# Query and key of differential heads: in the core, or by way of DRAM

## The chip, the cores and the metric

The kernel runs on one core of one Trainium2 chip. The time is device microseconds of one execution; runs are compared by their median. The engines named here are TensorE (PE), VectorE (DVE), ScalarE (ACT), GpSimd (POOL) and SyncE (SP), which issues all DMAs of this kernel.

## What is computed

Two layers over 1040 tokens (16 meta tokens and 1024 inputs), model width 1024. In each layer a normalised input is projected into two groups of heads: four differential pairs (two maps of width 64 each, with partial rotary embedding) and eight forgetting heads (no rotary):

```python
def partial_rope(t, cos, sin):          # ROT_DIM = 16 of HEAD_DIM = 64
    half = ROT_DIM // 2
    t1, t2, tp = t[..., :half], t[..., half:ROT_DIM], t[..., ROT_DIM:]
    ...
    return jnp.concatenate([t1 * cos - t2 * sin, t2 * cos + t1 * sin, tp], axis=-1)
...
dq = partial_rope(dq.reshape(b, lp, DIFF_HEADS, 2, HEAD_DIM), cos, sin)
dk = partial_rope(dk.reshape(b, lp, DIFF_HEADS, 2, HEAD_DIM), cos, sin)
...
p = jax.nn.softmax(s, axis=-1)
a = p[:, :, 0] - lam * p[:, :, 1]       # the two maps of a pair
```

So of the 128 rows of q or k of a pair only 2 x 16 are rotated; the other 96 pass as they are. Each pair's output is normalised, gated by a SiLU path, and all heads go through one output projection that is added to the residual.

## The kernel before

**Tiling.** Tokens lie along the free axis in three chunks of 336, 384 and 320 (`CS`, `CE`), and in nine blocks for attention. All float32 products are made of float32r parts: an operand is split into a high part (a rounded copy, on ACT) and a low part (the rest, on DVE), and a projection tile (`mtile`) is 24 matmuls: eight k tiles times high x high, low x high, high x low. A score sums two products: k's tile holds the highs of one map in its 64 rows and the lows in the other 64, `qq` holds q's highs twice (the second copy by POOL, L477), `ql` the lows.

**Units.** A layer's side work is cut into units: `k_unit`, `q_unit` and `gate` (one pair, three chunks, one `mtile` each), `v_unit` (two pairs, nine blocks of 24 matmuls). `attention` goes pair by pair (0 to 3 differential, 4 to 7 forgetting), chunk by chunk: scores, softmax, transposes, products with v. PE's order is set by a planner: `ORDER` lists the units, `fills` runs them as filling between the steps of `attention`, and due times tell it how long after its last matmul a tile may be used (`LROT`, 8.0 us for rotated ones, `LFOX` for the others, in `when`). The other engines' and SP's order is set by the framework's scheduler, engine by engine, from the same program; each engine, and SP, takes its list in order.

**Rotation** (`rotate`, L407 to 422), once per unit and chunk on 128 rows: a DMA of a full table of cosines and sines (L413), a copy out of PSUM on ACT (L416), a shuffle that swaps the halves of the rotated rows (DVE, L418), the product with the sines (POOL, L419), the product with the cosines and the add (DVE, L420, L421); rows that aren't rotated meet a one and a zero. Then `split` by halves of 64 rows (L426, L428).

**Buffers.** `WB` 8 converted weight tiles, `XB` 4 staging tiles for loaded weights (`load_w`, L244: 128 KB each, high on ACT or POOL, low on POOL or DVE), `QB` 8 q tiles, `GB` 4 kept gates, `TCB` 3 work tiles. The output projection (`out_main`) loads its weights again for each chunk: 8 x 3 x 4 loads a layer. PSUM has two banks for projections (`pj`), three for scores (`sc`).

## Time and profile before

| | us |
|---|---|
| median of 3 runs (lowest, highest) | 1605.58 (1605.05, 1609.21) |
| the profiled execution's own time | 1607.66 |
| its span, first to last instruction | 1605.6 |
| PE busy in the span | 1487.7 |
| DVE busy | 1043.0 |

The mean granted clock of PE is 0.973 of full speed. Durations below come from the one profiled execution. A span leaves out 2.1 us of the execution's own time. Busy time of PE is modelled from pipelined matmuls, so what counts is where it sits idle and what ended that. The differential pairs of layer 0 lie at 86 to 350 us, those of layer 1 at 850 to 1140; forgetting heads, output projection and the next layer's first units follow each.

### The profile page before, as it was taken

Reading aid. Unit: us, or ns where it says so; the run is one execution under the profiler, and the core shown is the slowest. Engines: PE = TensorE matmul, PEld = TensorE weight load, DVE = VectorE, ACT = ScalarE, POOL = GpSimd, SP = SyncE. Lnnn points to the kernel's source line nnn. Section 1 sums busy time; section 2 is a strip of 40 time slices with the busy share of each in tenths; the row PEclk is TensorE's granted clock in tenths of the full one; section 3 lists DMA queues with packets and bytes.
Section 4 is the critical chain, followed back from the end, with each engine's and each line's share of the span. In section 5 each row is a group of like instructions: output and inputs, shape, how many; then the busy total and the mean of one; then the engine's idle time right before and its main releaser. Section 6 shows DMA issues by size and latency. Waiting matters only on the chain. (4 is left out here: it accounts for less than half of the span.)

```text
span 1605.6 us, 30162 instructions
## 1 busy us (share of the span) xinstructions
PE 1487.7 (93%) x9932; PEld 1420.1 (88%) x9932; DVE 1043.0 (65%) x3024; ACT 828.6 (52%) x2067; POOL 689.6 (43%) x1125
## 2 busy tenths in 40 slices
PE   5988999999999999988998999899999999888997
PEld 4888989999999999887988899799999999886897
DVE  6488747866755575757655976586756555547564
ACT  6455545545654565543334654465556556446443
POOL 3353233404442445456846341442253344344674
PEclk9999999999999999998999999999999999999999
DMA  9252212223321324555434231332242222335454
GB/s 242 64 113 73 71 51 75 72 36 86 69 66 42 79 67 126 170 151 159 147 70 106 69 87 33 88 81 50 43 93 59 52 69 61 87 96 159 138 158 139
DMA packets 181725, 148.28 MB, mean 92 GB/s; under 512 B 19624, under 2 KB 177120, under 8 KB 181568
## 3 DMA queue, kind: packets, MB, share of 16 engines
q1 hardware_dynamic: 181568, 146.34, 34.6%
q8 instruction: 79, 1.29, 0.3%
q14 instruction: 78, 0.64, 0.1%
...
## 5 line engine op out<-in xcount | busy, mean ns | idle before, releaser
L179 PE MATMUL pj<-acth,whi 128*128 128x320 f32 (+2 forms) x1536 | 517.0, 337 | 22.9 <-ACT tc L416 7.6
L179 PE MATMUL pj<-acth,wlo 128*128 128x320 f32 (+2 forms) x1536 | 498.1, 324 | 2.7 <-POOL wlo L263 2.7
L179 PE MATMUL pj<-actl,whi 128*128 128x320 f32 (+2 forms) x1536 | 497.8, 324 | 0.0
L263 POOL TENSOR_TENSOR wlo<-wst,whi 128x256 fp32r<-128x256 f32 (+1 forms) x320 | 249.3, 788 | 244.0 <-ACT whi L259 216.3
L179 PEld LDWEIGHTS pj<-acth,whi 128*128 128x128 f32 x1536 | 295.9, 193 | 28.0 <-ACT tc L416 8.2
L179 PEld LDWEIGHTS pj<-acth,wlo 128*128 128x128 f32 x1536 | 295.2, 192 | 3.8 <-POOL wlo L263 3.2
L179 PEld LDWEIGHTS pj<-actl,whi 128*128 128x128 f32 x1536 | 293.9, 191 | 0.0
L660 ACT ACTIVATE e<-e,mn 80x80 f32<-80x80 f32 (+8 forms) x288 | 225.2, 782 | 124.2 <-DVE mn L652 121.6
L744 DVE TENSOR_TENSOR atl<-tp,ath 128x320 fp32r<-128x320 f32 (+8 forms) x432 | 191.5, 450 | 97.7 <-ACT ath L743 92.9
L743 ACT ACTIVATE ath<-tp 128x320 fp32r<-128x320 f32 (+8 forms) x432 | 167.6, 403 | 138.2 <-PE tp L183 131.1
L179 PE MATMUL sc<-kt,qq 128*128 128x296 f32 (+9 forms) x480 | 178.8, 375 | 25.2 <-DVE mn L652 17.3
L259 ACT ACTIVATE whi<-wst 128x256 fp32r<-128x256 f32 (+1 forms) x304 | 124.1, 415 | 150.4 <-DMA wst<-in_w_out_dram 50.7
L693 POOL TENSOR_SCALAR e<-e,rl 80x80 f32<-80x80 f32 (+2 forms) x144 | 110.8, 770 | 165.6 <-DVE rl L692 160.2
L183 PE MATMUL tp<-ident,e 128*128 128x128 f32 (+2 forms) x1080 | 180.7, 275 | 0.9 <-POOL e L693 0.8
L179 PE MATMUL po<-ath,v 128*128 128x256 f32 (+5 forms) x576 | 167.1, 331 | 13.2 <-ACT ath L743 9.9
L179 PE MATMUL pj<-whi,acth 128*128 128x256 f32 (+3 forms) x576 | 166.4, 289 | 6.7 <-DVE v L428 5.8
L179 PE MATMUL pj<-wlo,acth 128*128 128x256 f32 (+3 forms) x576 | 164.2, 285 | 2.1 <-POOL wlo L263 1.4
L179 PE MATMUL pj<-whi,actl 128*128 128x256 f32 (+3 forms) x576 | 163.8, 284 | 0.6 <-POOL actl L404 0.6
L179 PE MATMUL sc<-kt,ql 128*128 128x296 f32 (+9 forms) x480 | 159.7, 335 | 0.0
L179 PE MATMUL po<-atl,v 128*128 128x256 f32 (+5 forms) x432 | 136.8, 317 | 12.8 <-DVE atl L744 11.7
L183 PEld LDWEIGHTS tp<-ident,e 128*128 128x128 f32 (+2 forms) x1080 | 137.1, 140 | 7.0 <-POOL e L693 2.3
L179 PEld LDWEIGHTS sc<-kt,qq 128*128 128x128 f32 (+1 forms) x480 | 91.5, 191 | 37.7 <-DVE mn L652 23.8
...
## 6 DMA issues: line engine op xcount, KB each, us to landing
wst<-in_w_in_dram SPq DMA_DIRECT2D x256, 128.0 KB
wst<-in_w_out_dram SPq DMA_DIRECT2D x192, 128.0 KB
...
```

The lines of the kernel that those rows point to most:

```text
L179: nc.tensor.matmul(o, a, b, start=start, stop=stop)
L183: nc.tensor.transpose(o, a, idn)
L259: nc.scalar.activation(hi, sg_, AF.Copy)
L263: eng.tensor_tensor(lo, sg_, hi.bitcast(F32), ALU.subtract)
L660: nc.scalar.activation(e[rows, :ext], e[rows, :ext], AF.Exp, scale=-1.0, bias=mn[rows, len(pcs) - 1:len(pcs)], accum_out=l[rows, :])
L693: nc.gpsimd.tensor_scalar(e[rows, :ext], e[rows, :ext], r[rows, 0:1], 1.0, ALU.mult, ALU.mult)
L743: nc.scalar.activation(ah[:kz, n0:w], tp[:kz, n0:w], AF.Copy)
L744: nc.vector.tensor_tensor(al[:kz, n0:w], tp[:kz, n0:w], ah[:kz, n0:w].bitcast(F32), ALU.subtract)
```

## The change

For pairs 0 to 3 `k_unit` and `q_unit` hand over to a new `diff_unit`. Per chunk it copies the tile out of PSUM, stores its 2 x 16 raw rotated rows to DRAM (`rscr`), splits all 128 rows at once into highs and lows (`ks`), and stores the 2 x 48 rows that aren't rotated to DRAM (`qkscr`). When q and k of a pair both have a chunk, `rotate` loads their 64 raw rows into one tile, rotates and splits these alone, and stores them to `qkscr` in eight DMAs. `diff_loads` then loads k (four DMAs; chunk by chunk for pair 0, whole for the others), `qq` (two) and `ql` (two) from there. The table for 64 rows is laid out in DRAM once (`rtab`, eight copies). The planner has new due times (`LROT` 9.0, `LBACK` 2.5 after it), another `ORDER`, and `log_forget` is placed by `LLF`. q of the differential heads no longer skips 16 columns in layer 1. Buffers: `XB` 3, `QB` 6 (in pairs), `GB` 2, `TCB` 4, `KB` 2 new.

```diff
-WB, XB, QB, EB, AB, GB, OB, TCB = 8, 4, 8, 6, 2, 4, 3, 3
+WB, XB, QB, EB, AB, GB, OB, TCB, KB = 8, 3, 6, 6, 2, 2, 3, 4, 2
...
-ORDER = ("k0 q0 k1 q1 | g0 k2 v1 q2 | g1 k3 q3 | g2 v2 k4 q4 | g3 k5 q5 | g4 v3 h k6 q6 | k7 q7 g5 | "
+ORDER = ("k0 q0 k1 q1 | k2 q2 v1 | g0 k3 q3 | k4 v2 q4 | g1 g2 k5 q5 | g3 v3 h k6 q6 | g4 k7 q7 g5 | "
          "g6 g7")
...
-LS, LSC, LT, L1S, LROT, LFOX = ((1.9, 0.0033), (3.4, 0.0042)), 0.7, 2.4, 4.87, 8.0, 5.61
+LS, LSC, LT, L1S, LFOX = ((1.9, 0.0033), (3.4, 0.0042)), 0.7, 2.4, 4.87, 5.61
+LTO, LROT, LBACK = 4.0, 9.0, 2.5
+LLF = 8.0
...
-SHUF = list(range(8, 16)) + list(range(8)) + list(range(16, 32))
+SHUF = list(range(8, 16)) + list(range(8)) + list(range(24, 32)) + list(range(16, 24))
...
+        for r in range(0, P, 16):
+            dma(out=rtab[r:r + 16], in_=rope[0:16])
...
-    def rotate(pt, c, scale, o=0):
-        a, b = CS[c] + o, CE[c]
-        w = b - a
-        rt = sb.tile([P, T], F32, name="cb", tag="cb", bufs=2)[:, 0:2 * w]
+    def rotate(l, g, c):
+        a, b = CS[c], CE[c]
+        w, n = b - a, 32 * len(ROPED[g])
+        rt = sb.tile([P, T], F32, name="cb", tag="cb", bufs=2)[:n, 0:2 * w]
         rt = rt.rearrange("p (x w) -> p x w", x=2)
-        dma(out=rt, in_=rope[:, :, a:b])
-        t = st("tc", CW)
-        v = t[:, o:o + w]
-        nc.scalar.activation(v, pt[:, o:o + w], AF.Copy, scale=scale)
-        t2 = st("tc", CW)
-        nc.vector.stream_shuffle(t2[:, :w], v, SHUF)
-        nc.gpsimd.tensor_tensor(t2[:, :w], t2[:, :w], rt[:, 1, :], ALU.mult)
+        dma(out=rt, in_=rtab[:n, :, a:b])
+        v, t2 = st("tc", CW)[:n, :w], st("tc", CW)[:n, :w]
+        dma(out=v, in_=rscr[l, g][:, a:b])
+        nc.vector.stream_shuffle(t2, v, SHUF)
+        nc.gpsimd.tensor_tensor(t2, t2, rt[:, 1, :], ALU.mult)
         nc.vector.tensor_tensor(v, v, rt[:, 0, :], ALU.mult)
-        nc.vector.tensor_tensor(v, v, t2[:, :w], ALU.add)
-        return t
+        nc.vector.tensor_tensor(v, v, t2, ALU.add)
+        split(t2.bitcast(F32R), v.bitcast(F32R), v)
+        for r in range(0, n, 16):
+            i, m = divmod(r // 16, 2)
+            for x, t in enumerate((t2, v)):
+                dma(out=qkscr[l, g][i, 64 * m:64 * m + 16, x, a:b], in_=t[r:r + 16, :])
+    def diff_unit(l, u, acts, box):
+        scale, c0 = (-SCALE, DQ) if u[0] == "q" else (1.0, DK)
+        c0 += int(u[1]) * P
+        g, i = WHERE[u]
+        ws = load_w_all(w_in[l], [(c0, c0 + P)])
+        for c in range(3):
+            a, b = CS[c], CE[c]
+            w = b - a
+            mb = []
+            yield from mtile(ws, acts, c, mb)
+            pt = mb[0][:, :w]
+            v = st("tc", CW)
+            nc.scalar.activation(v[:, :w], pt, AF.Copy, scale=scale)
+            for m in range(2):
+                dma(out=rscr[l, g][32 * i + 16 * m:32 * i + 16 * m + 16, a:b],
+                    in_=v[64 * m:64 * m + 16, :w])
+            parts = sb.tile([P, 2, CW], F32R, name="ks", tag="ks", bufs=KB)[:, :, :w]
+            split(parts[:, 0, :], parts[:, 1, :], pt, scale)
+            for m in range(2):
+                r = slice(64 * m + 16, 64 * m + 64)
+                dma(out=qkscr[l, g][i, r, :, a:b], in_=parts[r].bitcast(F32))
+            box["to", u, c] = pe.t + LTO
+            if all(("to", x, c) in box for x in ROPED[g]):
+                rotate(l, g, c)
+                box["at", g, c] = pe.t + LROT
+            diff_loads(l, box)
+            yield
+    def diff_loads(l, box):
+        while box["lk"] < 12:
+            p, c = divmod(box["lk"], 3)
+            g, i = WHERE[f"k{p}"]
+            if ("at", g, c if p == 0 else 2) not in box or box.get("sp", 0) < p - 1:
+                break
+            if c == 0:
+                box["kt"] = [big("kt", 4, F32R) for _ in range(2)]
+            cols = slice(CS[c], CE[c]) if p == 0 else slice(0, T)
+            if p == 0 or c == 0:
+                for s in range(2):
+                    for x in range(2):
+                        dma(out=box["kt"][s][halves(s)[x], cols].bitcast(F32),
+                            in_=qkscr[l, g][i, halves(s)[0], x, cols])
+                box["lt"] = max(pe.t, box["at", g, c if p == 0 else 2]) + LBACK
+            box["k", p, c] = box["kt"]
+            when["k", p, c] = box["lt"]
+            box["lk"] += 1
+        while box["lq"] < 12:
+            p, c = divmod(box["lq"], 3)
+            g, i = WHERE[f"q{p}"]
+            if ("at", g, c) not in box or p and (p - 1, c) not in box["sc_ok"]:
+                break
+            a, b = CS[c], CE[c]
+            qq = sb.tile([P, 2, CW], F32R, name="qq", tag="qq", bufs=QB // 2)
+            ql = qls[c]
+            for r in halves(0):
+                dma(out=qq[r, :, 0:b - a].bitcast(F32),
+                    in_=qkscr[l, g][i, :, 0, a:b].rearrange("(m d) w -> d m w", d=HD))
+            for s in range(2):
+                r = halves(s)[0]
+                dma(out=ql[s][r, :].bitcast(F32), in_=qkscr[l, g][i, r, 1, a:b])
+            box["q", p, c] = ([qq[:, s, :] for s in range(2)], ql)
+            when["q", p, c] = max(pe.t, box["at", g, c]) + LBACK
+            box["lq"] += 1
...
-            src = rotate(mb[0], c, 1.0) if diff else mb[0]
             for s in range(2):
                 r, ro = halves(s)
-                split(kt[s][r, a:b], kt[s][ro, a:b], src[r, :w])
+                split(kt[s][r, a:b], kt[s][ro, a:b], mb[0][r, :b - a])
...
-            while box["kept"] >= GB:
+            while box["kept"] >= (GB - 1 if p == 7 and c else GB):
```

**SP at pair 0.** SP's list before, from the last table of k0 on: `cb` is the table, `wst` a staging tile of weights.

```order
L413 DMA cb_940<-in_rope_dram 128x2x320
L413 DMA cb_1002<-in_rope_dram 128x2x336
L252 DMA wst_1411<-in_w_in_dram 128x2x128
L252 DMA wst_1417<-in_w_in_dram 128x2x128
L252 DMA wst_1423<-in_w_in_dram 128x2x128
L252 DMA wst_1429<-in_w_in_dram 128x2x128
L413 DMA cb_1044<-in_rope_dram 128x2x384
L413 DMA cb_1086<-in_rope_dram 128x2x320
L413 DMA cb_1211<-in_rope_dram 128x2x336
```

SP's list now, from the raw rows of q0's chunk 0 on (`r00` and `s00` are layer 0, pair 0; `tc` rotated rows, `ks` the others):

```order
L461 DMA r00_111<-tc_1005 16x336 x2
L467 DMA s00_103<-ks_1009 96x1x336 x2
L434 DMA tc_1016<-r00_111 64x336
L461 DMA r00_111<-tc_1069 16x384 x2
L432 DMA cb_1140<-rtab_119 64x2x320
L467 DMA s00_103<-ks_1073 96x1x384
L444 DMA s00_103<-tc_1017 16x336 x2
L444 DMA s00_103<-tc_1016 16x336 x2
L444 DMA s00_103<-tc_1017 16x336
L444 DMA s00_103<-tc_1016 16x336
L444 DMA s00_103<-tc_1017 16x336
L444 DMA s00_103<-tc_1016 16x336
```

Before, SP only brought tables and weights; now its list holds stores, a load that waits for them, and stores that wait for the rotation, and behind these stand `kt` (four), `qq` (two) and `ql` (two).

**SP at pair 3.** SP's list before, at the last tables of q3 and the first weights of v2 (`ta` and `oscr` belong to attention's outputs and gates):

```order
L252 DMA wst_3856<-in_w_in_dram 128x2x128
L786 DMA oscr_100<-ta_3269 128x336
L252 DMA wst_3862<-in_w_in_dram 128x2x128
L620 DMA oscr_100<-ta_3184 128x320
L413 DMA cb_3560<-in_rope_dram 128x2x320
L413 DMA cb_3668<-in_rope_dram 128x2x336
L252 DMA wst_4081<-in_w_in_dram 128x256
L252 DMA wst_4081<-in_w_in_dram 128x8
```

SP's list now, from the loads of chunk 1 to the last transfer ahead of chunk 2's rotated rows:

```order
L507 DMA ql10_87<-s03_106 64x384
L503 DMA qq_3767<-s03_106 64x2x384 x2
L507 DMA ql11_88<-s03_106 64x384
L461 DMA r03_114<-tc_3820 16x320 x2
L467 DMA s03_106<-ks_3824 96x1x320 x2
L434 DMA tc_3831<-r03_114 64x320
L268 DMA wst_4046<-in_w_in_dram 128x2x128
L268 DMA wst_4341<-in_w_in_dram 128x256
L268 DMA wst_4341<-in_w_in_dram 128x8
L268 DMA wst_4348<-in_w_in_dram 128x256
L268 DMA wst_4348<-in_w_in_dram 128x8
L710 DMA oscr_100<-ta_3883 128x336
```

The raw rows of chunk 2 stand behind chunk 1's loads, and weights and a gate's store between them and their own rotated rows; k of pair 3 (`kt`) comes behind all of it.

**DVE at pair 3.** DVE's list before, around q3's rotations of chunks 0 and 1 (`e`, `mn` are scores, `atl` lows of transposes):

```order
L418 STREAM_SHUFFLE tc_3672<-tc_3670 128x336
L712 SCALAR_TENSOR_TENSOR e_3581<-e_3626,rl_3638,e_3581 128x976
L420 TENSOR_TENSOR tc_3670<-tc_3670,cb_3668 128x336
L421 TENSOR_TENSOR tc_3670<-tc_3670,tc_3672 128x336
L803 COPY ms_809<-sc_3727 128x1
L418 STREAM_SHUFFLE tc_3714<-tc_3712 128x384
L803 COPY ms_809<-sc_3727 128x1 x2
L428 TENSOR_TENSOR ql00_85<-tc_3670,qq_3677 64x336
L420 TENSOR_TENSOR tc_3712<-tc_3712,cb_3710 128x384
L428 TENSOR_TENSOR ql01_86<-tc_3670,qq_3678 64x336
L744 TENSOR_TENSOR atl_3739<-tp_3734,ath_3738 80x320
L744 TENSOR_TENSOR atl_3747<-tp_3742,ath_3746 128x320
```

DVE's list now, around the rotations of chunks 1 and 2 (L705 empties the tiles of gate g1):

```order
L437 TENSOR_TENSOR tc_3750<-tc_3750,cb_3748 64x384
L438 TENSOR_TENSOR tc_3750<-tc_3750,tc_3751 64x384
L516 TENSOR_TENSOR tc_3750<-tc_3750,tc_3751 64x384
L518 SCALAR_TENSOR_TENSOR ks_3824<-pj_3795,ks_3824 128x320
L435 STREAM_SHUFFLE tc_3832<-tc_3831 64x320
L705 SCALAR_TENSOR_TENSOR tc_3910<-tc_3910,pj_3885 128x336
L437 TENSOR_TENSOR tc_3831<-tc_3831,cb_3829 64x320
L705 SCALAR_TENSOR_TENSOR tc_3942<-tc_3942,pj_3917 128x384
L438 TENSOR_TENSOR tc_3831<-tc_3831,tc_3832 64x320
L516 TENSOR_TENSOR tc_3831<-tc_3831,tc_3832 64x320
L705 SCALAR_TENSOR_TENSOR tc_3974<-tc_3974,pj_3949 128x320
L742 ISA e_3979,mn_3980<-sc_3981,dm0_69 80x80
```

The rotations have moved from among scores and transposes to the gate's three tiles, whose evictions now stand behind the shuffle of rows that come by DMA. On PE the three tiles of g1 (72 matmuls) are what stands between q3's last tile and the first score of pair 3; before, it was q3's own chunk 1 and half of chunk 2.

## Rows read from the trace of the kernel before

**Rows 1.** The page's part 1: busy us, share of span, instructions by engine.
```profile
PE 1487.7 (93%) x9932; PEld 1420.1 (88%) x9932; DVE 1043.0 (65%) x3024; ACT 828.6 (52%) x2067; POOL 689.6 (43%) x1125
```

**Rows 2.** Busy time by stretch: length; five engines; then clock, DMA share, GB/s.
```profile
86.00:350.00 264.00, 244.79 (x1645) 235.71 (x1644) 197.43 (x583) 139.12 (x354) 90.51 (x131) 0.98 0.29 70
...
850.00:1140.00 290.00, 268.91 (x1822) 260.42 (x1821) 209.52 (x629) 150.54 (x383) 102.57 (x161) 0.98 0.28 69
```

**Rows 3.** Waits of PE over the run: us in total, times, longest.
```profile
PE sc L179 <- DVE mn L652: 17.3, 15, 3.8
...
PE pj L179 <- ACT tc L416: 7.6, 2, 5.5
```

**Rows 4.** Groups by line: operands, count | busy us, mean ns | idle before.
```profile
L419 POOL TENSOR_TENSOR tc<-tc,cb 128x320 f32<-128x320 f32 (+2 forms) x48 | 57.8, 1204 | 66.0 <-issue 41.2 <-DVE tc L418 20.8 <-POOL qq L477 1.8
...
L420 DVE TENSOR_TENSOR tc<-tc,cb 128x320 f32<-128x320 f32 (+2 forms) x48 | 34.4, 717 | 2.7 <-DMA cb<-in_rope_dram 1.9
...
L421 DVE TENSOR_TENSOR tc<-tc 128x320 f32<-128x320 f32 (+2 forms) x48 | 29.7, 619 | 16.9 <-POOL tc L419 16.1
...
L428 DVE TENSOR_TENSOR kt<-tc,kt 64x336 fp32r<-64x336 f32 (+2 forms) x48 | 26.5, 552 | 5.2 <-ACT kt L426 3.9
L418 DVE STREAM_SHUFFLE tc<-tc 128x320 f32<-128x320 f32 (+2 forms) x48 | 26.2, 547 | 0.6
...
L426 ACT ACTIVATE kt<-tc 64x336 fp32r<-64x336 f32 (+2 forms) x48 | 23.5, 490 | 25.6 <-DVE tc L421 24.9
...
L416 ACT ACTIVATE tc<-pj 128x320 f32<-128x320 f32 (+2 forms) x48 | 21.8, 455 | 20.2 <-PE pj L179 19.4 <-DVE kt L428 0.3
```

**Rows 5.** Instructions in order of time, 82 to 92 us: start, length, engine, line.
```profile
83.72 0.45 ACT L416 ACTIVATE tc<-pj 128x336 f32<-128x336 f32 x1 [0.28 <-DVE kt L428]
...
86.11 0.54 DVE L418 STREAM_SHUFFLE tc<-tc 128x336 f32<-128x336 f32 x1
...
86.78 1.16 POOL L419 TENSOR_TENSOR tc<-tc,cb 128x336 f32<-128x336 f32 x1 [1.33 <-DVE tc L418]
...
87.19 1.12 DVE L420 TENSOR_TENSOR tc<-tc,cb 128x336 f32<-128x336 f32 x1
...
89.92 1.19 DVE L428 TENSOR_TENSOR ql<-tc,qq 64x336 fp32r<-64x336 f32 x2 [0.55 <-ACT qq L426]
```

**Rows 6.** SyncE's issues in order of time, 384 to 389 us.
```profile
386.14 0.34 SPq L577 DMA_DIRECT2D cscr<-cb  x1
387.95 0.83 SPq L819 DMA_DIRECT2D cb<-cscr  x2
```

**Rows 7.** SyncE's issues in order of time, 540 to 552 us.
```profile
545.69 3.56 SPq L895 DMA_DIRECT2D nscr<-msr  x12
```

**Rows 8.** The chain of waits that ended last: start, length, what.
```profile
1467.39 2.34 DMA oscr<-ta
...
1523.84 3.37 DMA tc<-nscr
...
1549.34 2.23 DMA wst<-in_w_out_dram
...
1583.28 10.55 PE pj L179 x72
```

**Rows 9.** PE's instructions in order of time, 737 to 744 us.
```profile
740.21 0.69 PE L179 MATMUL pj<-acth,whi 128*128 128x384 f32 x1 [1.90 <-DVE hc L930]
...
742.94 0.52 PE L179 MATMUL pj<-actl,whi 128*128 128x384 f32 x1
743.26 0.52 PE L179 MATMUL pj<-acth,whi 128*128 128x384 f32 x1
```

**Rows 10.** Groups by line, 700 to 760 us: the weights' conversions.
```profile
L263 POOL TENSOR_TENSOR wlo<-wst,whi 128x256 fp32r<-128x256 f32 x22 | 17.2, 785 | 10.6 <-ACT whi L259 9.5 <-DMA wst<-in_w_out_dram 0.9
...
L261 POOL TENSOR_SCALAR whi<-wst 128x256 fp32r<-128x256 f32 x20 | 9.6, 485 | 8.7 <-DMA wst<-in_w_out_dram 6.5 <-DVE tc L914 0.6 <-ACT tc L938 0.5
L259 ACT ACTIVATE whi<-wst 128x256 fp32r<-128x256 f32 x21 | 8.7, 416 | 19.8 <-DMA wst<-in_w_out_dram 9.1 <-PE pj L179 7.2 <-POOL whi L261 2.7
```

More of the change, by code (lines that the diff above doesn't have):

```diff
@@ L157, in trunk_kernel @@
     cscr = dr.tile([depth, 8, T], F32, name="cscr")
+    qkscr = {(l, g): dr.tile([len(us), P, 2, T], F32, name=f"s{l}{g}")
+             for l in range(depth) for g, us in enumerate(ROPED)}
+    rscr = {(l, g): dr.tile([32 * len(us), T], F32, name=f"r{l}{g}")
+            for l in range(depth) for g, us in enumerate(ROPED)}
+    rtab = dr.tile([P, 2, T], F32, name="rtab")
     class Clock:
@@ L378, in first_turn @@
                 tr(pt[:, o:o + n], xts[b][:n, k * P:(k + 1) * P], ident[:n, :n])
-            h = hc_view(hc, c, k) if hc else st("qq", CW, F32, QB)[:, 0:w]
+            if not hc and k % 2 == 0:
+                two = sb.tile([P, 2, CW], F32, name="qq" if k < QB else "ks",
+                              tag="qq" if k < QB else "ks", bufs=QB // 2 if k < QB else KB)
+            h = hc_view(hc, c, k) if hc else two[:, k % 2, 0:w]
             nc.scalar.activation(h, pt[:, :w], AF.Copy)
@@ L435, in k_unit @@
     def k_unit(l, p, acts, box):
-        diff = p < 4
-        k0 = (DK if diff else FK) + (p % 4) * P
+        if p < 4:
+            yield from diff_unit(l, f"k{p}", acts, box)
+            return
+        k0 = FK + (p % 4) * P
         while box.get("sp", 0) < p - 1:
@@ L444, in k_unit @@
             a, b = CS[c], CE[c]
-            w = b - a
             mb = []
             yield from mtile(ws, acts, c, mb)
-            src = rotate(mb[0], c, 1.0) if diff else mb[0]
             for s in range(2):
                 r, ro = halves(s)
-                split(kt[s][r, a:b], kt[s][ro, a:b], src[r, :w])
+                split(kt[s][r, a:b], kt[s][ro, a:b], mb[0][r, :b - a])
             box["k", p, c] = kt
-            when["k", p, c] = pe.t + (LROT if diff else LFOX)
+            when["k", p, c] = pe.t + LFOX
             yield
     def q_unit(l, p, acts, box):
-        diff = p < 4
-        q0 = (DQ if diff else FQ) + (p % 4) * P
+        if p < 4:
+            yield from diff_unit(l, f"q{p}", acts, box)
+            return
+        q0 = FQ + (p % 4) * P
         ws = load_w_all(w_in[l], [(q0, q0 + P)])
@@ L463, in q_unit @@
             w = CE[c] - CS[c]
-            while p and (p - 1, c) not in box["sc_ok"]:
+            while (p - 1, c) not in box["sc_ok"]:
                 yield True
@@ L467, in q_unit @@
             yield from mtile(ws, acts, c, mb, o)
-            src, scale = (rotate(mb[0], c, -SCALE, o), 1.0) if diff else (mb[0], -SCALE)
-            qq = [st("qq", CW, F32R, QB) for _ in range(2)]
+            qq = sb.tile([P, 2, CW], F32R, name="qq", tag="qq", bufs=QB // 2)
+            qq = [qq[:, s, :] for s in range(2)]
             ql = qls[c]
@@ L475, in q_unit @@
                 r, ro = halves(s)
-                split(qq[s][r, o:w], ql[s][r, o:w], src[r, o:w], scale)
+                split(qq[s][r, o:w], ql[s][r, o:w], mb[0][r, o:w], -SCALE)
                 nc.gpsimd.tensor_scalar(qq[s][ro, o:w], qq[s][r, o:w].bitcast(F32), 1.0, 1.0,
@@ L1040, in fills @@
                         other, r = None, True
+                if "lf" in box and pe.t > box["lft"]:
+                    box.pop("lf")()
                 yield r
-            if "lf" in box and u[0] not in "vh":
-                box.pop("lf")()
+            if u[0] in "vh":
+                box["lft"] = pe.t + LLF
             if other is not None and (not todo or todo[0][0] == "v"):
@@ L1115, in trunk_kernel @@
         acts = [None] * 3
-        box = {"done": {}, "sc_ok": set(), "fin": set(), "kept": 0, "sums": 0}
+        box = {"done": {}, "sc_ok": set(), "fin": set(), "kept": 0, "sums": 0, "lk": 0, "lq": 0}
         v0 = v_unit(0, 0, acts, box)
@@ L1141, in trunk_kernel @@
             if l < depth - 1:
-                acts, box = new, {"done": {}, "sc_ok": set(), "fin": set(), "kept": 0, "sums": 0}
+                acts, box = new, {"done": {}, "sc_ok": set(), "fin": set(), "kept": 0, "sums": 0, "lk": 0, "lq": 0}
                 v0 = weave(v_unit(l + 1, 0, acts, box), tail)
```

7 lines of the change are left out of this document (5 added, 2 removed).

## The prediction

> **What bounds the kernel now.** I read the page's busy line first, then busy time by stretch, then the waits of TensorE, then groups by line, then SyncE's issues in order of time. TensorE (PE) is busy 93% of the span, the next engine, VectorE (DVE), 65% [rows 1]: only PE's idle time can be won, and any PE wait is lost. The change works in two stretches, the differential heads of layer 0 (86 to 350 us) and of layer 1 (850 to 1140 us). There PE is idle 264.0 - 244.8 = 19.2 and 290.0 - 268.9 = 21.1 us, at a mean granted clock of 0.98 [rows 2]. So 40.3 us is all that faster side engines could return. What ends those waits is mostly DVE emptying score banks (17.3 us in the whole run); only the 7.6 us for L416, the copy in front of the rotation, names the rotary path itself [rows 3].
>
> **What is removed.** Per unit (k or q of a pair) and chunk there was one copy, shuffle, two products, an add, and highs and lows by halves; now there is a copy and one split of all 128 rows, and per pair and chunk (24 instead of 48) one rotation of 64 rows. DVE before, at the means of [rows 4]: 48 x (0.547 + 0.717 + 0.619) + 96 x 0.552 = 143 us. After, with the same 0.552 for the split of 128 rows: 24 x (0.547 + 0.717 + 0.619 + 0.552) + 48 x 0.552 = 85 us. So 58 us leave DVE, and half of L419, 29 us, leaves GpSimd (POOL), beside its copies of q highs. ScalarE: 48 x 0.455 + 96 x 0.490 = 69 us becomes 96 x 0.455 + 24 x 0.490 = 55. None of this is on PE, so it is worth only the PE waits that it ends: between 0 and 40.3 us. I take 20: the 7.6 us of L416 and a bit over a third of the other 33, since DVE keeps its 24 rotations and the score work that ends most waits is untouched. PE itself gains 16 columns x 96 matmuls in layer 1 (the skipped columns of chunk 0), 0.7 us at 10.55 us / (72 x 320) a column [rows 8]; left out of the sum.
>
> **What is added: two trips through DRAM, all on SyncE's (SP's) one queue.** The new chain from the last matmul of q's chunk to the first score is: copy; two stores of 16 rows; load of the rotated rows; rotation and split; eight stores; loads of k and q. Each hop waits for the landing of the one before it, and SP takes its list in order. Prices, low and high:
> - copy 0.455 [rows 4];
> - the second store of the pair is issued 0.30 later (12 small stores took 3.56 us of SP [rows 7]) and lands after 1.81 (a 33 KB store at 386.14, the load that reads it issued at 387.95 [rows 6]) or 2.34 us [rows 8]: 2.11 to 2.64;
> - load 2.23 (a weight load, the shortest hop in the chain) to 3.37 [rows 8];
> - rotation and split 0.547 + 1.204 + 0.619 + 0.490 + 0.552 = 3.41 [rows 4], or 4.4 with what queues between (86.11 to about 90.5 in the kernel before [rows 5]);
> - eight stores 7 x 0.30 + 1.81 = 3.91, to 4.44;
> - seven loads until the first score has all it reads (four of k, two of q, one of its lows): 6 x 0.30 + 2.23 = 4.03, to 5.17.
> Sum 16.2 to 20.5 us.
>
> A page of the Trainium skill speaks against this form: "DMA: Bandwidth & Descriptors", Rules for kernel authors, says to coalesce many small transfers, since under 64 KB one pays mostly overhead. The trace agrees as far as it goes: the 33 KB store costs 1.81 us, one of 80 to 96 KB 2.34. By the rule, two stores for eight would take 6 x 0.30 = 1.8 us off each chain; no run here shows that.
>
> **What covers it.** PE's order is fixed, so the cover is the PE work that stands between q's tile and the first score. At pair 0 it is three tiles of 24 matmuls: 72 of 320 columns took 10.55 us [rows 8], at the mean width of 347 it is 11.4 us. Before, it was two tiles, about 7.7 us, and the in-core chain just fitted (copy at 83.72, last low written about 90.5 [rows 5]).
> - Pair 0, chunk 0: 16.2 - 11.4 = 4.8, to 9.1 us of stall.
> - Pair 0, chunk 1: in SP's list its load of rotated rows stands behind all loads of chunk 0. From landing to landing: 3 x 0.30 + 3.41 + 3.91 + 4.03 = 12.3 us (14.9 high: 0.9 + 4.4 + 4.44 + 5.17). Between the two first scores PE has 36 projection matmuls, 12 of scores, 5 transposes, about 8 us: stall 4.3 to 6.9. Chunk 2 has 15 us of cover: none.
> - Pair 1: 66 matmuls and 6 transposes of cover, again 11.4; k is loaded whole, so only two loads stand ahead (1.5 less), but larger ones: 14.7 to 20.5, stall 3.3 to 9.1.
> - Pair 2: eight tiles of v1 (192 matmuls) stand between: none.
> - Pair 3: only the three tiles of g1, 11.4 us, and the three chunks are strung up. In SP's list the stores of chunk 2's raw rows stand behind chunk 0's and chunk 1's stores and loads. From the end of chunk 0's tile: chunk 0 to its last issue 0.455 + 2.11 + 2.23 + 3.41 + 3.91 + 1.2 = 13.3; chunk 1's stores and loads 3.91 + 1.2 = 5.1; chunk 2 2.11 + 2.23 + 3.41 + 3.91 + 2.53 = 14.2; together 32.6. PE has 8.6 (chunks 1 and 2) + 11.4: stall 12.6. With the high prices and the six weight and gate transfers that stand between (0.30 each): 22.5. DVE's list has g1's evictions behind the shuffle of chunk 2, so PE also runs out of banks before it comes to the score; that is the same wait, met earlier.
> Per layer 25.0 to 47.6. I take 36, the middle: the bare sums have no queueing, and before, 3.9 us of bare operations took 6.8. Two layers: **+72 us** (50 to 95).
>
> **After each stall** the clock falls: at 740.21, after 1.90 us idle, matmuls of 384 columns start 0.32 us apart instead of 384 x 0.458 ns = 0.176, the lower of the two levels (1.2 against 2.4 GHz), for ten of them [rows 9]: 1.45 us. Four stalls a layer: **+12** (0 to 12).
>
> **Buffers.** Staging of weights (XB) goes from four slots to three. In the output projection, 700 to 760 us, 21 + 20 loads were converted [rows 10], 1.46 us each, while PE's tile wants four in 3.5 to 4.2 us. A slot so turns in 4 x 1.46 = 5.9 us; if that stays, three slots give 1.95 us a load, 0.49 more; if it can shrink to load, high and low (2.23 + 0.42 + 0.79 = 3.4 us), nothing. Of 96 loads a layer the last 64 have no attention beside them: 0 to 2 x 31 us. I take **+13**, a fifth, since a slot's turn also holds waits for the eight converted tiles, which stay eight. Gate buffers (GB) go from four to two, so g7's last two tiles (4 us each) can't run ahead of their attention: 0 to 16, taken **+6**, since they still have to be run and only lose their place as cover. In the other stretches weights are wanted four per 25 us; three slots hide there. The larger DMA volume hides beside DMA engines that are 0.28 to 0.29 busy [rows 2].
>
> **Sum:** 72 + 12 - 20 + 13 + 6 = +83 on the span of 1605.6. The profiled execution took 1607.66, 2.1 over the median of 1605.58; the difference goes on the median: **1689 us**.
>
> **Rivals.**
> - *The relief wins (faster).* If a trip through DRAM is shorter than the 11.4 us of cover, no score waits for it, and the freed DVE and POOL end waits: 1605.6 - 20 = 1586. For it: DVE is what PE waits for in these stretches. Against: four hops of 1.81 to 2.23 us alone are 8.1, with the rotation 11.5, before any issue is counted. A lock between DVE and POOL would make the relief larger: the product of L420 took 1.12 us at 87.19 beside POOL's L419 from 86.78 [rows 5], where the mean is 0.717; with all 40.3 us back it is 1565. The Trainium skill has it so ("SBUF — State Buffer", Who interferes with whom: DVE and GpSimd share a port pair as an exclusive lock), and that row agrees.
> - *Stalls and relief cancel:* low chain prices in both layers, full relief: within 0.3%.
> - *Only the staging costs.* Chains are hidden, but three slots turn as slowly as four: 1605.6 - 20 + 50 = 1636.
> - *Worse than summed.* SP's list also has stores of attention outputs, and DVE's has score evictions behind shuffles; if each of the 24 rotations blocks these, high prices hold everywhere: 1605.6 + 95 + 12 + 40 + 16 = 1769.
> - That the rotations aren't halved is excluded: the built order has 24 shuffles where it had 48.
>
> **How the numbers follow.** Forecast (1632 to 1755) 0.76, relief wins 0.09, cancel 0.03, staging alone 0.05, worse 0.07. The range is the forecast's own: from +26 (low chain prices, most of the relief) to +149 (high ones, half the staging bound), and it leaves out the first two rivals and the last, 0.19. 0.3% is about what a measurement of this kernel can tell from none. Faster 0.09, within 0.3% 0.03, slower 0.88.
>
> **What would show it.** PE waits for kt, qq or ql with a DMA as releaser, some 5 us or more, at the first scores of pairs 0, 1 and 3 and none at pair 2, the longest at pair 3; idle in the two stretches up from 40 to about 100 us; waits for DVE mn and ACT tc down. In the output stage, whi and wlo waits of PE above the few microseconds of before. It is wrong if the first scores of pair 3 come without a wait.

## The result, and the profile after

The changed kernel takes 1790.0 us (median, 1787.6 to 1796.2) against 1607.4 for the kernel before in the same runs: 1.114 times as long, 95% interval 1.111 to 1.117. Slower was right; +183 us instead of +83 lies outside the range of 1632 to 1755. The profiled execution has a span of 1790.0 us, 184.4 over the 1605.6 of before; that is the sum taken apart here. First the page's busy line, which answers to [rows 1]:

```profile
PE 1547.9 (86%) x9932; PEld 1459.7 (82%) x9932; DVE 981.5 (55%) x2904; ACT 809.8 (45%) x2043; POOL 624.4 (35%) x1035
```

PE has the same 9932 matmuls, is idle 124.2 us more (1790.0 - 1547.9 against 1605.6 - 1487.7), and its busy time grows by 60.2, for the same work. DVE gives back 61.5 us (58 predicted), POOL 65, ACT 19; what PE has of that is the second row of the table further on.

Next, busy time by stretch between the same marks of the program, before and then after (columns as in [rows 2]): each layer's differential stretch up to the forget gate's running sums, and the stretches from the first sums of squares of an output projection to the last (layer 0) or to the end (layer 1).

```profile
86.00:381.00 295.00, 275.16 (x1856) 265.32 (x1854) 221.79 (x659) 156.91 (x397) 101.38 (x148) 0.98 0.28 68
...
737.60:828.60 91.00, 79.94 (x476) 76.94 (x475) 61.36 (x132) 33.60 (x81) 63.27 (x86) 0.92 0.50 138
828.60:1159.00 330.40, 308.45 (x2105) 298.62 (x2105) 234.89 (x698) 170.89 (x435) 121.64 (x187) 0.98 0.28 67
...
1525.40:1605.60 80.20, 69.02 (x458) 67.90 (x456) 45.87 (x102) 34.10 (x71) 47.18 (x70) 0.97 0.49 148
```

```profile
86.00:438.30 352.30, 280.76 (x1799) 268.76 (x1797) 194.28 (x612) 147.53 (x383) 69.57 (x110) 0.90 0.41 99
...
817.50:928.00 110.50, 90.89 (x475) 78.88 (x474) 58.48 (x128) 32.07 (x79) 62.28 (x88) 0.90 0.38 108
928.00:1316.20 388.20, 317.42 (x2032) 304.54 (x2031) 205.92 (x637) 160.06 (x418) 82.24 (x131) 0.90 0.39 94
...
1696.80:1790.00 93.20, 74.57 (x458) 73.02 (x456) 45.60 (x104) 35.16 (x73) 47.64 (x73) 0.90 0.42 128
```

The differential stretches have 51.7 and 48.8 us more idle time. Their busy time, with 57 and 73 fewer matmuls (the three tiles of gate g2, 72 matmuls, now come behind the mark; 0.159 us a matmul at the mean width), is 14.7 and 20.6 us above what it should be, at a granted clock of 0.90 against 0.98. The output ends are 19.5 and 13.0 us longer at equal counts. What PE waits for, over the run (answers to [rows 3]):

```profile
PE pj L195 <- DVE ks L518: 27.6, 9, 4.8
PE pj L195 <- DVE ks L516: 19.7, 4, 7.9
...
PE sc L195 <- issue: 15.2, 2, 7.7
...
PE sc L195 <- DMA kt<-s: 14.1, 6, 6.6
PE pj L195 <- DVE tc L705: 13.7, 2, 6.9
PE sc L195 <- DMA qq<-s: 12.1, 2, 7.1
...
PE sc L195 <- DMA tc<-in_cst_dram: 9.2, 1, 9.2
...
PE sc L195 <- DVE ffz L649: 8.5, 1, 8.5
...
PE sc L195 <- DVE mn L742: 4.0, 6, 1.4
```

And where, in layer 0: PE's instructions in order of time, the first after each long wait (idle time and releaser in brackets).

```profile
97.37 0.42 PE L195 MATMUL pj<-acth,whi 128*128 128x336 f32 x1 [3.23 <-DVE ks L518]
...
110.00 0.47 PE L195 MATMUL sc<-kt,qq 128*80 128x256 f32 x1 [7.13 <-DMA qq<-s]
...
114.61 0.69 PE L195 MATMUL pj<-acth,whi 128*128 128x384 f32 x1 [2.65 <-DVE ks L518]
...
129.31 0.63 PE L195 MATMUL pj<-acth,whi 128*128 128x320 f32 x1 [7.88 <-DVE ks L516]
...
181.20 0.41 PE L195 MATMUL pj<-acth,whi 128*128 128x320 f32 x1 [2.52 <-DVE ks L516]
...
191.83 0.47 PE L195 MATMUL sc<-kt,qq 128*80 128x256 f32 x1 [7.72 <-issue]
...
327.56 0.42 PE L195 MATMUL pj<-acth,whi 128*128 128x336 f32 x1 [2.56 <-DVE ks L518]
...
336.20 0.69 PE L195 MATMUL pj<-acth,whi 128*128 128x384 f32 x1 [4.67 <-DVE ks L518]
...
349.43 0.63 PE L195 MATMUL pj<-acth,whi 128*128 128x320 f32 x1 [6.93 <-DVE tc L705]
...
361.32 0.47 PE L195 MATMUL sc<-kt,qq 128*80 128x256 f32 x1 [6.09 <-DMA kt<-s]
...
438.31 1.08 PE L195 MATMUL sc<-tc,ffz 80*8 80x80 f32 x5 [8.54 <-DVE ffz L649]
```

("issue" is a releaser that the profile doesn't show; that score is the first of pair 1.) Pair 0 has four of these (20.9 us), pair 1 two (10.2), pair 3 four (20.3); layer 1 has 20.1, 9.0 and 19.8. The last row is a wait that the prediction did not have: the matmuls of the forget gate's sums, in both layers (8.5 and 9.2).

### The profile page after: what moved, and what is told of

Its sections match the earlier page's. It is cut to its first block, busy times and chain, and to the rows that moved or that the text cites. A ratio compares the mean times of both kernels' runs of the same rounds, so it can differ in the third digit from the quotient of the medians.

```text
span 1790.0 us, 30775 instructions
## 1 busy us (share of the span) xinstructions
PE 1547.9 (86%) x9932; PEld 1459.7 (82%) x9932; DVE 981.5 (55%) x2904; ACT 809.8 (45%) x2043; POOL 624.4 (35%) x1035
## 4 chain that ended last, share of the span: by engine, by line
PE 49%; DMA 16%; DVE 11%; issue 9%; SPq 7%; POOL 4%; ACT 2%; POOLq 0%; DVEq 0%; ACTq 0%
PE pj L195 30%; PE sc L195 7%; PE po L195 6%; PE tp L199 5%; DMA wst<-in_w_in_dram 4%; DMA wst<-in_w_out_dram 4%; SPq L444 2%; POOL wlo L279 2%; DMA r<-tc 1%; DVE tc L420 1%; DMA tc<-nscr 1%; DMA kt<-s 1%; DVE wlo L279 1%; DVE e L742 1%; DMA actl<-oscr 1%
## 5 line engine op out<-in xcount | busy, mean ns | idle before, releaser
L195 PE MATMUL pj<-acth,whi 128*128 128x320 f32 (+2 forms) x1536 | 530.9, 346 | 75.4 <-DVE ks L518 27.6
L195 PE MATMUL pj<-acth,wlo 128*128 128x320 f32 (+2 forms) x1536 | 511.2, 333 | 18.4 <-DVE wlo L279 13.6
L195 PE MATMUL pj<-actl,whi 128*128 128x320 f32 (+2 forms) x1536 | 506.7, 330 | 0.0
L195 PEld LDWEIGHTS pj<-acth,whi 128*128 128x128 f32 x1536 | 304.6, 198 | 85.2 <-DVE ks L518 30.1
L279 POOL TENSOR_TENSOR wlo<-wst,whi 128x256 fp32r<-128x256 f32 (+1 forms) x320 | 245.1, 771 | 312.4 <-ACT whi L275 255.5
L195 PEld LDWEIGHTS pj<-acth,wlo 128*128 128x128 f32 x1536 | 304.3, 198 | 27.4 <-DVE wlo L279 18.4
L195 PEld LDWEIGHTS pj<-actl,whi 128*128 128x128 f32 x1536 | 302.4, 197 | 0.0
L195 PE MATMUL pj<-whi,acth 128*128 128x256 f32 (+3 forms) x576 | 170.5, 296 | 15.5 <-DVE v L516 8.3
L195 PE MATMUL po<-ath,v 128*128 128x256 f32 (+5 forms) x576 | 168.8, 334 | 12.2 <-ACT ath L833 7.4
L783 POOL TENSOR_SCALAR e<-e,rl 80x80 f32<-80x80 f32 (+2 forms) x144 | 109.8, 763 | 179.9 <-DVE rl L782 178.3
L195 PE MATMUL pj<-wlo,acth 128*128 128x256 f32 (+3 forms) x576 | 168.0, 292 | 2.8 <-POOL wlo L279 1.4
```

Source lines behind the costliest of these rows:

```text
L195: nc.tensor.matmul(o, a, b, start=start, stop=stop)
L279: eng.tensor_tensor(lo, sg_, hi.bitcast(F32), ALU.subtract)
L783: nc.gpsimd.tensor_scalar(e[rows, :ext], e[rows, :ext], r[rows, 0:1], 1.0, ALU.mult, ALU.mult)
```

## The experiments

All medians stand against 1790 us for the changed kernel and 1604 to 1607 for the one before.

**Scores cut from their chain.** The loads read an earlier pair's scratch, everything else stays (`earlier` is the pair before, or the last pair of layer 0).

```diff
-                            in_=qkscr[l, g][i, halves(s)[0], x, cols])
+                            in_=earlier(l, g)[i, halves(s)[0], x, cols])
...
```

> The changed kernel, in which the loads of k and q for the scores read what an earlier pair has stored (the first pair of layer 0 alone still reads its own). All stores, rotations and loads are still there in the same places; only the dependence of a score on its own chain is gone, so the numbers computed are not the reference's. In the changed kernel PE waits about 100 us around the first scores of pairs 0, 1 and 3 of both layers: some 45 us of it at scores (sc), some 61 us at projections for a bank that DVE has yet to empty (pj for ks and tc). Theory A, the chain is longer than its cover and all these waits are that one wait, met earlier or later: about 80 us go (the first pair of layer 0 stays) and 20 us or more of low clock with them, 1680 to 1700 us. Theory B, the waits for banks come from lists taken in order (DVE's evictions stand behind a shuffle that waits for the load of the rotated rows, SP's weights behind stores of a chain): the waits at scores go, about 30 us and their clock, and the pj waits stay, 1745 to 1765 us.

1726.7 us: 63 go, halfway between the two theories. Pair 3 of layer 0 now waits 2.0 (for ks), 3.1 (ks) and 2.8 us (tc) instead of 20.3; pair 0 of layer 1 waits 10.4 instead of 20.1, for banks alone. So at these pairs about half or more is the chain, and 8 to 10 us a pair is waits for banks that don't hang on the scores' own chain. Pair 1 has no such rest: 6.7 us for weights in layer 0 (ACT whi, at 177.49), no long wait in layer 1. Of the 79.4 us of waits outside the first pair, 46 are gone.

**More cover ahead of pair 0.**

```diff
-LTO, LROT, LBACK = 4.0, 9.0, 2.5
+LTO, LROT, LBACK = 4.0, 20.0, 2.5
```

> The changed kernel with one number of the planner changed: the time that it counts for a rotation, 9 to 20 us. PE's list then has 72 more projection matmuls (11.4 us) between q's tile and the first score of pair 0 in both layers, and 36 fewer before pair 1; pair 3 stands as it did. In the changed kernel pair 0 waits 20.9 us in layer 0 and 20.1 in layer 1: 3.2, 7.1, 2.7 and 7.9 us, and alike. Theory A (chain against cover): with 11.4 us more cover the waits at pair 0 all but go, about 30 us and 8 to 15 us of low clock, 1745 to 1755 us. Theory B (lists taken in order): only the 7.1 and 5.0 us at the first scores go, and the waits for banks, which stand behind shuffles, stay or come elsewhere: 1770 to 1785 us.

1823.4 us, 33 worse, which neither theory had. The first score no longer waits; the projections put ahead of it do, in PE's order of time:

```profile
114.41 0.69 PE L195 MATMUL pj<-acth,whi 128*128 128x384 f32 x1 [10.62 <-DVE ks L518]
...
140.12 0.69 PE L195 MATMUL pj<-acth,whi 128*128 128x384 f32 x1 [9.00 <-DVE ks L516]
...
240.15 0.50 PE L195 MATMUL pj<-whi,acth 128*80 128x256 f32 x1 [12.18 <-ACT whi L275]
```

Pair 0 waits 24.0 us instead of 20.9, and v1, which lost fill work in front of it, 12.2 for its weights instead of 3.4. Cover that stands in PE's order is cover only as long as its banks (two for projections) are emptied.

**Banks emptied by ACT alone**, without and with that cover (the second has both edits).

```diff
-            split(parts[:, 0, :], parts[:, 1, :], pt, scale)
+            nc.scalar.activation(parts[:, 0, :], pt, AF.Copy, scale=scale)
+            nc.gpsimd.tensor_tensor(parts[:, 1, :], v[:, :w], parts[:, 0, :].bitcast(F32),
+                                    ALU.subtract)
...
-        split(t2.bitcast(F32R), v.bitcast(F32R), v)
+        nc.gpsimd.tensor_scalar(t2.bitcast(F32R), v, 1.0, 1.0, ALU.mult, ALU.mult)
+        nc.gpsimd.tensor_tensor(v.bitcast(F32R), v, t2, ALU.subtract)
```

> The changed kernel, in which no bank of a projection waits for DVE: the lows of k's and q's tiles are taken by POOL from the copy in SBUF, and highs and lows of the rotated rows by POOL too, so that ACT alone empties the bank and has nothing of the rotation in its list. PE's order is the same. Theory A, the banks are only where PE meets a chain that is longer than its cover: PE's waits for ks go (47 us) but its waits at the first scores grow by as much, 1775 to 1800 us. Theory B, DVE's and ACT's lists are a limit of their own: the waits for ks go and come back by less than half, 1740 to 1765 us.

> The same, with the planner's time of a rotation at 20 us in place of 9, so that 72 more projection matmuls (11.4 us) stand ahead of the first score of pair 0. With the lists as they were, this order took 1823 us in place of 1790: the score no longer waited, but the projections put ahead of it did (24 us at pair 0, for banks, and 12 to 13 us for v1's weights). Theory B, cover can't be used because projections empty their banks through lists that the rotation blocks: with the banks free, pair 0's 20 to 24 us all but go, 1740 to 1765 us, below the same edit with little cover. Theory A, the lists are not it (SP's or the weights' are): above 1790 us.

1783.5 and 1790.0 us. Without more cover theory A holds: waits for ks fall from 47 to 10 us, and the first score of pair 0 waits 15.0 instead of 7.1. With more cover the same edit is worth 33 us (1823 to 1790): pair 0's waits for DVE are gone, but ACT's highs (ks L465) now make PE wait 63 us, 16 times. So cover still doesn't pay: 1790.0 with it, 1783.5 without, where theory B had it below. What holds ACT can be read there: its copies into `tc` waited 42.0 us for stores of rotated rows, six times and up to 12.3 us, and its highs 19.0 us for stores of ks. The four and two slots of tc and ks stay taken until stores in SP's list have landed. No run gave them more slots.

**The forget gate's sums at their delay.** `lft` was left over from v1 when v2's last tile set `lf`.

```diff
-                box["lf"] = log_forget(l, z)
+                box["lf"], box["lft"] = log_forget(l, z), pe.t + LLF
```

> The changed kernel with the forget gate's running sums taken at the delay that the change means (8 us after the last tile of v2 by the planner's count); in the changed kernel the time is left over from the unit before, so they stand right behind that tile. PE waits 8.5 and 9.2 us there, and 10.2 us of low clock follow each time. Theory A, the place of the sums in PE's order is the cause: both waits go and most of their low clock, 18 to 28 us, 1762 to 1772 us. Theory B, the wait only moves (attention of the next pair needs the sums as soon): less than 6 us, 1784 to 1790 us.

1782.7 us, 7 less; between the two. The waits of 8.5 and 9.2 us fall to 1.1 at most; 3.9 and 3.7 come back some 12 us later, at transposes that wait for POOL (e L783).

**Staging slots and gate buffers, in the kernel before**: first XB 3 alone, then XB 3 and GB 2 (with the rule for the last gate tiles), then XB 7 paid for with QB 6.

```diff
-WB, XB, QB, EB, AB, GB, OB, TCB = 8, 4, 8, 6, 2, 4, 3, 3
+WB, XB, QB, EB, AB, GB, OB, TCB = 8, 3, 8, 6, 2, 4, 3, 3
```

> The kernel before with three staging slots for weights (XB) in place of four, and nothing else. The prediction had +13 us for this (0 to 63), all in the output projection. In the changed kernel the stretch from the first to the last sum of squares of layer 0 (out projection and first tiles of layer 1) takes 110.5 us against 91.0, and the last stretch of the run 93.2 against 80.2. Theory A, the staging slots are the cause of both: +25 to +35 us, 1632 to 1642 us, with PE's waits for whi and wlo up from about 10 us to 35 or more. Theory B, three slots hide and those stretches are longer for another reason: within 5 us of 1607.

> The kernel before with three staging slots and with two gate buffers in place of four (and the rule that the last gate tiles wait for a buffer more): with three slots alone it took 1644.6 us. The prediction had 6 us (0 to 16) for the gate buffers: 1645 to 1660 us; at nothing 1640 to 1648.

> The kernel before with seven staging slots for weights instead of four, paid for with two of the eight q tiles. Going from four to three cost 38.6 us. If a slot's turn sets the pace of the output projection also at four, 10 to 30 us go, 1575 to 1595 us; if four is where it is hidden, 1600 to 1612 us.

1644.6 us: +38.6 for one slot, a little above theory A. PE's waits from 690 to 860 us, first before, then with three slots:

```profile
PE pj L179 <- ACT whi L259: 2.9, 2, 2.3
...
PE pj L179 <- DVE wlo L263: 0.4, 1, 0.4
```

```profile
PE pj L179 <- DVE wlo L263: 9.6, 11, 2.2
...
PE pj L179 <- POOL whi L261: 4.0, 5, 2.7
```

The two gate buffers cost nothing that can be told (1641.5). Seven slots give 1582.2 us, 0.986 of the kernel before (0.984 to 0.988), so this version beats both kernels. Its gain is not where I expected it: the two output ends together are 1.7 us shorter, the differential stretches 7.5 and 12.0, in which the waits for ACT's copy in front of the rotation (2.1 and 5.5 us, L416) are gone. The two numbers, seven slots and six q tiles, were not tried apart.

**Staging in the changed kernel**, six slots, paid for with one attention tile.

```diff
-WB, XB, QB, EB, AB, GB, OB, TCB, KB = 8, 3, 6, 6, 2, 2, 3, 4, 2
+WB, XB, QB, EB, AB, GB, OB, TCB, KB = 8, 6, 6, 5, 2, 2, 3, 4, 2
```

> The changed kernel with six staging slots for weights in place of three, paid for with one of six attention tiles (e). In the kernel before, three for four cost 38.6 us and seven for four gave 22. If staging costs the changed kernel as much: 35 to 60 us go, 1730 to 1755 us, most of it in the two stretches of the output projection (110.5 and 93.2 us). If the changed kernel's stalls elsewhere hide it, or the fifth tile costs as much: 1770 us or more.

1741.2 us, 49 less: the two output ends take 87.0 and 82.7 us instead of 110.5 and 93.2. That is 34.0 of the span's 53.0 us; the other 19.0 come from the stretches between, where the prediction had three slots hide. Of the 53.0, 37.6 is PE's busy time, for the same matmuls.

**Number and form of the transfers.** First two stores for eight; then also whole tiles for the raw and the split rows and three loads of k for four (a_few), the same with more cover and free banks (a_few_ev20), and the whole tiles (a_few2) and the loads of k (a_fewk) apart, each with the two stores.

```diff
-        for r in range(0, n, 16):
-            i, m = divmod(r // 16, 2)
-            for x, t in enumerate((t2, v)):
-                dma(out=qkscr[l, g][i, 64 * m:64 * m + 16, x, a:b], in_=t[r:r + 16, :])
+        for x, t in enumerate((t2, v)):
+            dma(out=qkscr[l, g].rearrange("i (m d) x w -> (i m) d x w", m=2)[:, 0:16, x, a:b],
+                in_=t)
...
-                for s in range(2):
-                    for x in range(2):
-                        dma(out=box["kt"][s][halves(s)[x], cols].bitcast(F32),
-                            in_=qkscr[l, g][i, halves(s)[0], x, cols])
+                dma(out=box["kt"][0][:, cols].bitcast(F32),
+                    in_=qkscr[l, g][i, 0:64, :, cols].rearrange("d x w -> x d w"))
...
+            dma(out=rscr[l, g][i, :, a:b], in_=v[:, :w])
...
+            dma(out=qkscr[l, g][i, :, :, a:b], in_=parts.bitcast(F32))
```

> The changed kernel with the eight stores of 16 rotated rows as two of 64 rows. In the trace of the changed kernel eight take 3.55 to 3.81 us of SP, 0.46 each, not 0.30 as the prediction had it, and the loads behind them 0.60 each. If the issue of many small transfers on SP's one list is what makes a chain longer than priced: 6 x 0.46 = 2.8 us off every chain, two of them in a row at pair 0, one at pair 1, three at pair 3, 16.6 us per layer and some clock with it: 1745 to 1765 us. If landings and lists of other engines set the chain: within 10 us of 1790.

> The changed kernel with fewer and larger transfers for the same trips: two stores of 64 rotated rows for eight, whole tiles of 128 rows for the raw and the split rows (one store each for two), and three loads of k for four: 15 instead of 26 transfers for each chunk of pair 0. Eight stores as two alone gave 24 us (1766). In the changed kernel SP issues for 43.8 of the 51.8 us from 93.2 to 145.0. If SP's issuing is what sets the distance of two chunks (16.2 and 14.6 us at pair 0), the waits of chunk 1 at pair 0 and of pair 3 shrink again: 1735 to 1755 us. If the landings do (two for each trip, whatever their number), it stays at 1760 to 1770.

> The same with fewer transfers, with the banks emptied by ACT alone and with 72 more matmuls ahead of the first score of pair 0. That cover and free banks alone left 63 us of waits for ACT's highs (ks), 16 of them: the slots of ks and tc are still held by transfers in SP's list. If it is SP's list that ties the banks, most of these waits and pair 0's go: 1715 to 1740 us, below fewer transfers alone. If not, as fewer transfers alone or above, 1750 to 1775 us.

> Fewer transfers again, but with the four loads of k as they were: two stores of 64 rotated rows, whole tiles of 128 rows for the raw and the split rows; 16 transfers for a chunk of pair 0 in place of 26. With k in three loads it took 1825 us. In that trace, after the last issue of pair 3's loads, one of 520 KB for k[0] is still under way for some 9 us, at 59 GB/s and a DMA share of 0.1. If that load is what cost it, SP's issue time is free to show: 1735 to 1762 us, at or below the 1766 of two stores alone. If whole tiles (more bytes, a store that the rotated rows must wait for) cost it, above 1790 us.

> Two stores of rotated rows (1766 us) and of the other edits only the three loads of k: k[0], highs on 64 rows and lows on 64 rows, by one transfer whose outer dimension is 2. If this load is slow because it runs on two of the sixteen DMA engines: 1800 to 1830 us. If not: 1755 to 1770 us.

Two stores alone: 1766.0 us, 24 less, 1 us outside what the first theory had. But the first score of pair 0 still waits 7.3 us (7.1 before): the loads of k now wait for the two stores to land, where they came right behind the eight. What shrinks is the wait at 129.31 (7.88), which becomes one of 1.9 and one of 1.5, and with it SP's order has changed. The load of chunk 2's raw rows (L434) stood behind chunk 1's loads of k in the changed kernel, and stands ahead of them with two stores:

```profile
119.87 2.41 SPq L488 DMA_DIRECT2D kt<-s  x4
...
124.97 0.59 SPq L434 DMA_DIRECT2D tc<-r  x1
```

```profile
117.71 0.52 SPq L434 DMA_DIRECT2D tc<-r  x1
119.98 2.72 SPq L487 DMA_DIRECT2D kt<-s  x4
```

Layer 1 has the same change. So the 24 us are not the price of six issues alone; two stores in the old order were not run. a_few: 1825.0, and a_few_ev20 1815.1; both theories missed each. a_few at pair 3, 369 to 386 us: DMA busy in tenths and GB/s in 40 slices, then the load, then PE's first score.

```profile
DMA  3103652288999999971285111011011010110201
GB/s 116 39 25 31 181 181 20 59 166 333 323 258 194 168 216 200 262 237 64 66 174 177 49 49 59 39 59 59 39 59 59 39 59 39 59 59 39 59 20 47
...
kt<-s SPq DMA_DIRECT2D x1, 520.0 KB
```

```profile
384.93 0.50 PE L195 MATMUL sc<-kt,qq 128*80 128x256 f32 x1 [15.97 <-DMA kt<-s]
```

From about 378.5 us on only a tenth of the DMA engines' time is used, at 39 to 59 GB/s, until PE's score comes at 384.93: the load whose outer dimension is 2. It costs 55 us by itself (a_fewk, 1821.1 against 1766.0). Without it (a_few2) 1780.2, between that run's two theories: ten fewer transfers a chunk, but whole tiles cost 14 us more than two stores alone. So the number of transfers was only part of it; SP's issuing is not the whole price of a chain.

**POOL issues the chain's transfers.**

```diff
-        dma(out=rt, in_=rtab[:n, :, a:b])
+        nc.gpsimd.dma_start(out=rt, in_=rtab[:n, :, a:b])
...
```

> The changed kernel with the transfers behind the rotation's start (table, rotated rows, eight stores, the loads of k and q) issued by POOL; weights, raw stores and attention outputs stay on SP. If SP's list, taken in order, is what holds raw stores and weights back (at pair 3 the raw stores of q's last chunk are issued 7.6 us after its copy, behind stores and loads of the chunk before): 20 to 45 us go, 1745 to 1770 us. If a transfer costs POOL more to issue than SP, or POOL's conversions of weights now stand behind the waits: 1800 us or more.

1809.3 us. The waits at projections of pair 0 shrink, but those at first scores are 12.3, 17.6 and 14.1 us at pairs 0, 1 and 3 of layer 0, and POOL is busy 189 us more.

**Three edits together**: two stores, the sums at their delay, six slots.

> Three of the edits together on the changed kernel: two stores of rotated rows (24 us alone), the forget gate's sums at their delay (7 us alone), six staging slots (35 to 60 expected). If the costs are separate and add: 1790 - 24 - 7 - 48 = 1711 us, 1695 to 1730; if they hide one another, 1735 us or more. What is left over 1607 then is the stall at the first scores and its clock.

1709.4 us against a sum of 1711 forecast from the parts (1710 by their measured values): these three gains add. What is left, 102 us over 1607, was not taken apart further; the scores cut from their chain gave 63 of the 183 by themselves.

## Where the prediction held and where it failed

Its +83 and the 184.4 of the span, term by term (the second row is what is left of PE's idle time when the others are counted):

| term | predicted | measured in the two traces |
|---|---|---|
| stalls around the first scores | +72 | +100.3 |
| other idle of the two stretches (relief) | -20 | -17.5 |
| PE busy longer, same stretches (clock) | +12 | +35.3 |
| forget gate's sums | none | +17.7 |
| rest of the run (staging, gates) | +19 | +48.6 |

The kind of wait and its places were right, and four terms were too small: the stalls by 28 us, the clock by 23, staging and the rest by 30, and the sums, put at nothing, by 18. The largest term, the stalls, failed at the price of the chain: hops were added up as if no list made them wait, and the middle of these bounds was taken.

- **Mechanism and places** were right: waits of 5 to 8 us at the first scores of pairs 0, 1 and 3, none at pair 2's scores (5 us at v1's weights and banks there); waits for DVE mn went from 17.3 to 4.0 us, those for L416 to none. Pair 3 was not the longest; pair 0 was, by little.
- **The stalls were sized too low.** Per pair, 20.9, 10.2 and 20.3 us were measured against bounds of 9.1 to 16.0, 3.3 to 9.1 and 12.6 to 22.5. The step that failed is adding up hops without queueing in ACT's and SP's lists and then taking the middle. Here are SP's issues of pair 0's first chunk, its raw rows from 90.17 on, then ACT's copy of it, then DVE's part of the rotation:

```profile
88.53 1.59 SPq L268 DMA_DIRECT2D wst<-in_w_in_dram  x2
90.17 0.92 SPq L461 DMA_DIRECT2D r<-tc  x2
...
93.25 0.49 SPq L434 DMA_DIRECT2D tc<-r  x1
...
99.88 3.55 SPq L444 DMA_DIRECT2D s<-tc  x8
103.48 2.39 SPq L488 DMA_DIRECT2D kt<-s  x4
```

```profile
88.47 0.42 ACT L275 ACTIVATE whi<-wst 128x256 fp32r<-128x256 f32 x1 [2.89 <-DMA wst<-in_w_in_dram]
88.79 0.43 ACT L459 ACTIVATE tc<-pj 128x336 f32<-128x336 f32 x1
```

```profile
95.79 0.52 DVE L435 STREAM_SHUFFLE tc<-tc 64x336 f32<-64x336 f32 x1
...
97.63 1.71 DVE L438 TENSOR_TENSOR tc<-tc 64x336 f32<-64x336 f32 x1 [0.32 <-POOL tc L436]
99.89 0.90 DVE L516 TENSOR_TENSOR tc<-tc 64x336 fp32r<-64x336 f32 x1 [0.55 <-ACT tc L514]
```

  The chain took 23.8 us, from the end of q's tile at 86.24 (as modelled) to the score at 110.00, against 16.2 to 20.5. Hop by hop:

  | hop | predicted | measured |
  |---|---|---|
  | end of the tile to the copy's start | 0 | 2.6 |
  | copy | 0.5 | 0.4 |
  | copy's end to the load of the raw rows | 2.1 to 2.6 | 4.0 |
  | that load | 2.2 to 3.4 | 2.5 |
  | rotation and split | 3.4 to 4.4 | 5.0 |
  | eight stores and the loads, to the score | 7.9 to 9.6 | 9.2 |

  ACT came late to the copy, since it stood at a conversion whose weights were issued at 82.66, behind raw stores in SP's list, and landed at 88.4. The raw stores then stood behind a load of weights that waited for a staging slot until 89.7. In the rotation the add (L438) took 1.71 us, 0.62 in [rows 4]. The price of an issue was too low as well: a small store takes 3.55 / 8 = 0.44 us of SP and a load of k 2.39 / 4 = 0.60, not 0.30. But at this first chunk that doesn't show, since SP went from the stores to the loads of k without a wait for landing. From chunk to chunk it counts: the eight loads of chunk 0 hold SP for 5.0 us (103.48 to 108.51; 2.4 at 0.30 each), and chunk 1's stores begin 16.2 us after chunk 0's, where 12.3 to 14.9 had been counted from chunk to chunk. The copy's delay alone doesn't decide, either: with six slots it starts at once, at 88.31, and the score again comes 23.6 us behind the tile: the raw rows go out at 91.31, behind other transfers, and their load at 95.70.
- **"The same wait, met earlier"** was right for the order as built (a_ev), but PE's order was wrong as a measure of cover: 72 more matmuls brought nothing but new waits.
- **The clock** was taken from one idle time of 1.9 us [rows 9], four times a layer. There were about ten long waits a layer, most of them longer. PE from 110 us on:

```profile
110.27 0.41 PE L195 MATMUL sc<-kt,ql 128*80 128x256 f32 x1
110.48 0.41 PE L195 MATMUL sc<-kt,qq 128*80 128x256 f32 x1
...
117.82 0.52 PE L195 MATMUL pj<-acth,whi 128*128 128x384 f32 x1
118.14 0.46 PE L195 MATMUL pj<-acth,wlo 128*128 128x384 f32 x1
...
118.61 0.34 PE L195 MATMUL pj<-acth,whi 128*128 128x384 f32 x1
118.79 0.34 PE L195 MATMUL pj<-acth,wlo 128*128 128x384 f32 x1
```

  256 columns stand 0.21 us apart at 110.27 and 384 columns 0.32 at 117.82, the lower level of 1.2 GHz; by 118.61 they stand 0.18 apart. Between lies another wait of 2.65 us (114.61), so PE worked 5.8 us at half speed behind the two waits and lost about 2.9, where the prediction had ten matmuls and 1.45.
- **Staging** was mis-sized: 13 predicted (0 to 63), 38.6 measured alone. A fifth of the bound was a guess. Of a layer's last 64 loads SP issued one every 1.28 us (layer 0) and 1.25 us (layer 1) with four slots, and every 1.49 and 1.41 with three; an unchanged turn would have given 1.71 and 1.67. So the turn shrank, but the price is nearer half of the bound than a fifth. Gate buffers: 6 predicted, nothing measured.
- **The sums** were missed: I read the order at the first scores only. The new order puts k4's tiles ahead of v2, and nothing stands between v2's last tile and the sums; before, it was the three tiles of k4. Moving them back gives 7 us net.
- **The rival "worse than summed"** (1769, chance 0.07) was nearest in time, and its mechanism, lists blocked at the rotations, is what the run with more cover shows.

Not settled: how the 8 to 10 us a pair that stay with the scores cut from their chain divide among SP's, DVE's and ACT's lists; what two stores for eight are worth in an unchanged order of SP's list; and what the new `ORDER`, six q tiles and four work tiles cost or give alone, since none of them was run apart.
